# Mixer A of block 1: q and k of a head group projected together, 512 columns wide, and the latent attention's products with v one head later in the order

## The chip, the cores and the metric

One Trainium2 chip, one of its cores. The metric is the device time of one execution, in microseconds (us). The core has a matrix engine (PE, with its weight loads listed apart as PEld), a vector engine (DVE), an activation engine (ACT), a general engine (POOL) and a queue that issues transfers (SP). They run side by side and wait for each other through semaphores. Matrix products land in PSUM, which this kernel uses as eight buffers of 128x512 numbers: four named `acc`, two `mps`, two `ops`.

## The reference

Two transformer blocks in a row over 512 tokens of width 1024, in 32-bit floats. Only the first block's mixers are touched by the change:

```
proj  = rms_norm(h) @ w_in
o_a   = mixer_dilated(qkv_a) @ w_o_a       # mixer A: 3 groups of 4 heads of 64, dilations 1, 4, 16
o_b   = mixer_mla(q_c, kv_c, k_pe) @ w_o_b # mixer B, latent attention: 8 heads, full softmax
mix   = (g_a * o_a + g_b * o_b) @ w_out    # g_a, g_b: sigmoid gates from proj
h     = h + rms_norm(mix)
```

In `mixer_dilated` the q and the k of every head are turned by a rotary embedding on their first 16 of 64 numbers, each group of heads attends within a window over its own stride, and the three groups are combined by the softmax of their log-sums. In `mixer_mla` q and k have 64 plain and 32 rotary numbers a head, and each head does `softmax(q k) v` over all 512 tokens. Behind it comes an MLP (1024 to 4096 to 1024), and then the second block, with four other mixers and its own MLP.

## The kernel before

Every large product is made three times to keep its precision: each operand is split into a rounded part (hi) and the rest (lo), and `mm3` (lines 320 to 322) adds hi·hi, hi·lo and lo·hi into one PSUM buffer. Weights come from memory as units of up to 128x1024 numbers. A unit is loaded into `wraw` (3 buffers), cast by ACT into `whi` (5 buffers, line 300) and subtracted by DVE into `wlo` (5 buffers, line 301). A buffer comes free when PE has done its last product with the unit.

The change lies in `mixers1`. PE's instructions there stand in the order of the code; the other engines' instructions are placed by a scheduler when the program is built, and each engine then works in its own fixed order. The parts of `mixers1` that matter:

- `proj_v` and `proj_qk` project mixer A's v, q and k of one group. For each of the four 128-token tiles `lin_tm` makes 24 products: 8 slices of the width, 3 products each, with the tokens as the loaded operand and the weights as the streamed one, 256 columns wide. ACT copies the result out with a scale into `tm` (line 852), POOL applies the rotary embedding, and later PE transposes it, two 128x128 pieces a tile (line 860) into an `mps` buffer. After every second tile ACT and DVE copy one half each of that buffer into qT or kT (line 867).
- `ItemA` is one step of mixer A's attention: scores (lines 971 to 978), softmax, `turn` (transposes of P into `mps`, line 1014, and their copy to PT) and `out` (products with v, line 1032).
- `ItemB` is one head's 128 queries in the latent attention: `scores` (line 1092), a maximum on DVE (line 1095), an exponential on ACT (line 1099), a scale on DVE (line 1101), `turn` (four transposes, line 1106, and a copy to PT by DVE for the even head and ACT for the odd one, line 1107), and `out` (line 1122), which does both heads of a pair when the odd one comes.
- `fill` interleaves blocks of projections between these items. A block's transposes run two blocks after it (`Fill(2)`).

The loop at the end of `mixers1` steps through 16 items of A and 32 of B. At item n it issues the scores, then some blocks of fill, then the turn of an earlier item and the products with v of one earlier still. For B the turn is two items behind, and `out` three.

Of the kernel before, what the change touches and what calls it, by code (L numbers as in the profile page):

```python
# [15 lines left out]
AF = mybir.ActivationFunctionType  # L16
# [17 lines left out]
def _units():  # L34

    u = {}
    qkv = {"q": 0, "k": 768, "v": 1536}

    def rows(k0, n):
        return [128 * (k0 + i) for i in range(n)]  # L40

    for g in range(3):
        for nm in ("q", "k", "v"):
            c = list(range(qkv[nm] + 256 * g, qkv[nm] + 256 * g + 256))
            if nm == "v" and g == 0:
                c += list(range(3072, 3104))
            for h, (k0, n) in enumerate(TMK[len(c)]):
                u[f"A{nm}{g}", h] = ("w_in", rows(k0, n), c)
    for m in range(6):
        u["Bz", m] = ("w_in", rows(0, 8), list(range(2304 + 128 * m, 2432 + 128 * m)))  # L50
    heads = lambda hs, w, c0, n: [w * h + c0 + i for h in hs for i in range(n)]
    u["uqr"] = ("mla_w_uq", rows(0, 4), heads(range(8), 96, 64, 32))
    u["uv"] = ("mla_w_ukv", rows(0, 2), heads(range(8), 128, 64, 64))
    for p in range(4):
        u["uq", p] = ("mla_w_uq", rows(0, 4), heads((2 * p, 2 * p + 1), 96, 0, 64))
        u["uk", p] = ("mla_w_ukv", rows(0, 2), heads((2 * p, 2 * p + 1), 128, 0, 64))
    for m in range(16):
        u["G", m] = ("w_in", rows(0, 8), list(range(3104 + 128 * m, 3232 + 128 * m)))
    for q in range(2):
        u["oa", q] = ("w_o_a", rows(0, 2), list(range(512 * q, 512 * q + 512)))  # L60
    for q in range(4):
        u["ob", q] = ("w_o_b", rows(0, 4), list(range(256 * q, 256 * q + 256)))
    def output(nm, w, ks):

        for f in range(2):
            for i in range(0, len(ks), 2):
                u[nm, f, i // 2] = (w, [128 * k for k in ks[i:i + 2]], list(range(512 * f, 512 * f + 512)))

    def grouped(nm, w, sizes):

        for g, n in enumerate(sizes):
            k0 = sum(sizes[:g])
            if g + 1 < len(sizes):
                output((nm, g), w, range(k0, k0 + n))
            else:
                for k in range(n):
                    u[(nm, g), k] = (w, rows(k0 + k, 1), list(range(D)))

    output("out", "w_out", range(8))
    for m in range(32):  # L80
        u["ff1", m] = ("w_ff1", rows(0, 8), list(range(128 * m, 128 * m + 128)))
    grouped("ff2", "w_ff2", FF1)

    for nm, c0 in (("s5u", 0), ("hq", 256), ("hf", 512), ("fq", 1280), ("fk", 1536), ("mq", 2052), ("mk", 2308)):
        for m in range(2):
            u[nm, m] = ("w_in_2", rows(0, 8), list(range(c0 + 128 * m, c0 + 128 * m + 128)))
    for nm, c0 in (("hi", 768), ("hg", 1024), ("fv", 1792), ("mv", 2564), ("mo", 2820)):
        c = list(range(c0, c0 + 256))
        if nm == "hi":
            c += list(range(2048, 2052)) + list(range(3076, 3084))  # L90
        for h, (k0, n) in enumerate(TMK[len(c)]):
            u[nm, h] = ("w_in_2", rows(k0, n), c)
    output("out2", "w_out_2", (0, 1, 2, 3, 6, 7, 4, 5))
    for m in range(22):
        u["gate", m] = ("w_ffn_gate_2", rows(0, 8), list(range(128 * m, 128 * m + 128)))
        u["up", m] = ("w_ffn_up_2", rows(0, 8), list(range(128 * m, 128 * m + 128)))
    grouped("down", "w_ffn_down_2", FF2)
    return u
# [123 lines left out]
def program(ctx: ExitStack, tc: tile.TileContext, A, out):  # L222
# [15 lines left out]
    @contextmanager  # L238
    def phase(name, **bufs):
        with ExitStack() as st:  # L240
            CTX.bufs = bufs
            for a, n in (("cp", "c"), ("sp", "s"), ("up", "u")):
                setattr(CTX, a, st.enter_context(tc.tile_pool(name=f"{n}_{name}", bufs=1, reuse_waits="tile")))
            yield

    def u(nm="u", dt=F32, tag="u"):
        if tag in GLOBAL:
            return gpool.tile([128, 512], dt, name=nm, tag=tag, bufs=GLOBAL[tag])
        return CTX.up.tile([128, 512], dt, name=nm, tag=tag, bufs=CTX.bufs[tag])
# [4 lines left out]
    def mps():  # L254
        return psum.tile([128, 512], F32, name="mps", tag="mps", bufs=2)
# [59 lines left out]
    def wrows(nm, n, eng=DVE):  # L315
        return ktiles([wload([(nm, h)], eng=eng)[0] for h in range(len(TMK[n]))], 0, n)
# [153 lines left out]
    def lin_tm(ps, xs, pick, w, c0, n):  # L470

        K = len(xs)
        for k in range(K):
            wh, wl = w[k]
            xh, xl = pick(xs[k][0]), pick(xs[k][1])
            mm3(ps, (xh, xl), (wh[:, c0:c0 + n], wl[:, c0:c0 + n]), k == 0, k == K - 1)
# [216 lines left out]
    def tokpick(j):  # L693
        return lambda a: a[:, 128 * j:128 * j + 128]
# [95 lines left out]
    def mixers1(xs, zs, r_tm, rho, RX, rp, maskb):  # L790
# [48 lines left out]
                    gather_v(g)  # L839
                yield turn  # L840

        def proj_qk(g, nm):
            us = wrows(f"A{nm}{g}", 256)
            res = QKV[g][nm] = [u(f"{nm}T", tag="g"), u(f"{nm}T", tag="g")]
            tps = {}
            for j in range(4):
                ps = acc()
                lin_tm(ps[:, 0:256], xs, tokpick(j), us, 0, 256)
                if j % 2 == 0:
                    tt = u("tm")  # L850
                t = tt[:, 256 * (j % 2):256 * (j % 2) + 256]
                ACT.activation(t, ps[:, 0:256], AF.Copy, scale=r_tm[:, j:j + 1])
                rope(t.rearrange("p (h d) -> p h d", h=4)[:, :, 0:16], rp("ropeA", j, 32), 16, POOL)

                def turn(j=j, t=t):
                    if j % 2 == 0:
                        tps[j] = mps().rearrange("p (a x) -> p a x", a=2)
                    tpv = tps[j - j % 2]
                    for a in range(2):
                        PE.transpose(tpv[:, a, 128 * (j % 2):128 * (j % 2) + 128], t[:, 128 * a:128 * a + 128], ident)  # L860
                    if j % 2:
                        for a in range(2):
                            dst, src = res[a][:, 128 * (j - 1):128 * (j + 1)], tpv[:, a]
                            if g:
                                dst = res[a].rearrange("p (r x) -> p r x", r=4)[:, :, 32 * (j - 1):32 * (j + 1)]
                                src = src.rearrange("p (x r) -> p r x", r=4)
                            (ACT.copy if a == 0 else DVE.tensor_copy)(dst, src)
                yield turn


# [278 lines left out]

        order = [0, 8, 1, 9, 2, 10, 3, 11, 4, 12, 5, 13, 6, 14, 7, 15]  # L1150
        for g in range(3):
            fill.plan.extend([proj_v(g), proj_qk(g, "q"), proj_qk(g, "k")])
        fill.plan.extend([mixed([proj_qr(), proj_vb()], (0, 0, 1, 0, 1, 0, 1, 1)), proj_pair(0)] + [gate(m, "g") for m in order[0:2]])
        fill(14)
        rows_b()
        shared_k()
        items = [ItemA(0, j, e) for j in range(4) for e in range(2)]
        items += [ItemA(g, j, e) for g in (1, 2) for j in (0, 2) for e in range(2)]
        items += [ItemB(p, i, e) for p in range(4) for i in range(4) for e in range(2)]
        fills = [2, 1, 2, 1, 2, 1, 2, 1] + [3] * 4 + [4, 4, 3, 2]  # L1160
        fills += [0] * 32
        turned = outed = 0
        for n in range(len(items) + 4):
            if n < len(items):
                if n >= 16 and (n - 16) % 8 == 0:
                    p = (n - 16) // 8
                    if p < 3:
                        fill.plan.append(proj_pair(p + 1))
                    else:
                        fill.plan.extend(gate(m, "z") for m in order[2:14])  # L1170
                if n >= 16:
                    items[n].scores()
                elif n % 2 == 0:
                    items[n].scores(items[n + 1])
                fill(fills[n] if n < 16 else 1 if n % 8 in (1, 3) or n >= 40 and n % 2 else 0)
            if n == 24:
                combine_a()
            lag = 1 if n < 16 else 2
            while turned < len(items) and turned <= n - lag:
                items[turned].turn()  # L1180
                turned += 1
            while outed < turned and outed <= n - lag - 1:
                items[outed].out()
                outed += 1
                if outed == 16:
                    weights_a()
# [1033 lines left out]
               [lambda: po.scaled(pre.r)])  # L2220

    hd = [dram.tile([T, D], F32, name=f"hd{i}") for i in range(3)]
    with phase("m1", u=10, z=12):
        carry = mix1(hd[0])
    s5 = S5()
    with phase("f1", u=3, hid=14, s5=6):
# [21 lines left out]
```

## Time and profile before

| | |
|---|---|
| median of 3 runs | 1525.47 us (1524.91 to 1526.32) |
| the profiled execution | 1524.67 us |
| its span, first to last instruction | 1522.9 us |
| PE busy | 1478.0 us, 97% |
| DVE, ACT, POOL busy | 52%, 38%, 16% |
| granted clock, mean | 0.989 |

The profile is of one execution. A row of the timeline gives the start and the length of an instruction, or of several alike. Matrix products are pipelined, so the lengths of neighbours overlap, and what one costs is the distance from its start to the next one's start. In square brackets stands how long the engine sat idle before the row, and what ended that. In the windows, each engine's busy time has its number of instructions behind it.

### The profile page before, as it was taken

The numbers are of one execution on the slowest core, as the hardware profiler recorded it, in microseconds if no ns is written. First come the engines' busy times: TensorE is split into PE (matmuls) and PEld (weight loads), VectorE is DVE, ScalarE is ACT, GpSimd is POOL, SyncE is SP. The second block draws the span as 40 slices with busy tenths as digits, with TensorE's granted clock in tenths as the row PEclk, the third lists the DMA queues.
The fourth block names the chain that finished last, engine by engine and source line by source line (L and its number), as shares of the span: only waits on it lengthen the run. The fifth ranks groups of instructions, "written<-read, shape, count | busy, mean of one in ns | idle before, by whom it ended". The sixth has DMA issues, their size and how long they took to land.

```text
span 1522.9 us, 21857 instructions
## 1 busy us (share of the span) xinstructions
PE 1478.0 (97%) x8516; PEld 1240.6 (81%) x8520; DVE 788.6 (52%) x1569; ACT 583.7 (38%) x1099; POOL 246.2 (16%) x514
## 2 busy tenths in 40 slices
PE   8999999999999999999998999889999999999997
PEld 7999976678888888888887999667788888888885
DVE  6433367743746533434446686857656441434446
ACT  7344454533325442423225343533535323222222
POOL 0321210000201377203700052411000000000000
PEclk9999999999999999999999999979999999999999
DMA  8332121022225332322324423001124322423232
GB/s 302 132 100 75 45 64 42 33 80 97 90 91 179 119 97 70 119 85 87 110 93 141 146 88 116 32 29 42 42 90 161 124 97 59 136 83 111 83 97 84
DMA packets 54728, 147.37 MB, mean 97 GB/s; under 512 B 9824, under 2 KB 16368, under 8 KB 54624
## 3 DMA queue, kind: packets, MB, share of 16 engines
q1 hardware_dynamic: 52384, 143.38, 28.8%
q10 hardware_dynamic: 1776, 1.85, 0.4%
q8 instruction: 67, 1.10, 0.3%
q0 software_dynamic: 464, 0.74, 0.2%
q14 instruction: 37, 0.30, 0.1%
HBM read 135.12 MB, written 11.06 MB: 96 GB/s over the span
## 4 chain that ended last, share of the span: by engine, by line
PE 87%; DVE 9%; ACT 3%; issue 1%; DMA 1%; SPq 0%; DVEq 0%; ACTq 0%
PE acc L320 25%; PE acc L321 24%; PE acc L322 24%; DVE wlo L301 1%; PE acc L1092 1%; PE ops L1032 1%; PE ops L1122 1%; DVE y L625 1%; PE ops L320 1%; PE ops L322 1%; PE ops L321 1%; ACT whi L300 1%; PE acc L1977 1%; PE ops L1993 1%; PE acc L978 1%
## 5 line engine op out<-in xcount | busy, mean ns | idle before, releaser
L300 ACT CAST whi<-wraw 128x1024 fp32r<-128x1024 f32 (+4 forms) x237 | 234.5, 993 | 486.3 <-PE acc L321 226.6
L301 DVE TENSOR_TENSOR wlo<-wraw,whi 128x1024 fp32r<-128x1024 f32 (+4 forms) x237 | 282.2, 1195 | 233.7 <-ACT whi L300 224.1
L320 PE MATMUL acc<-xh,whi 128*128 128x512 f32 (+1 forms) x920 | 348.4, 380 | 7.2 <-ACT whi L300 5.3
L322 PE MATMUL acc<-xh,wlo 128*128 128x512 f32 (+1 forms) x920 | 343.5, 374 | 1.5 <-DVE wlo L301 1.5
L321 PE MATMUL acc<-xl,whi 128*128 128x512 f32 (+1 forms) x920 | 344.6, 375 | 0.3 <-DVE xl L664 0.3
L320 PEld LDWEIGHTS acc<-xh,whi 128*128 128x128 f32 x920 | 174.4, 190 | 44.1 <-ACT whi L300 7.5
L322 PEld LDWEIGHTS acc<-xh,wlo 128*128 128x128 f32 x920 | 174.2, 189 | 33.3 <-DVE wlo L301 2.1
L321 PEld LDWEIGHTS acc<-xl,whi 128*128 128x128 f32 x920 | 174.6, 190 | 31.7 <-issue 1.0
L320 PE MATMUL acc<-whi,hidh 128*128 128x512 f32 x432 | 169.0, 394 | 0.0
L321 PE MATMUL acc<-wlo,hidh 128*128 128x512 f32 x432 | 168.7, 393 | 0.0
L322 PE MATMUL acc<-whi,hidl 128*128 128x512 f32 x432 | 168.4, 392 | 0.0
L320 PE MATMUL acc<-whi,xh 128*128 128x256 f32 (+2 forms) x448 | 131.3, 293 | 0.2 <-ACT mv L1779 0.2
L321 PE MATMUL acc<-wlo,xh 128*128 128x256 f32 (+2 forms) x448 | 127.9, 285 | 0.0
L322 PE MATMUL acc<-whi,xl 128*128 128x256 f32 (+2 forms) x448 | 127.7, 285 | 0.0
L321 PEld LDWEIGHTS acc<-wlo,hidh 128*128 128x128 f32 x432 | 81.2, 188 | 18.3
L322 PEld LDWEIGHTS acc<-whi,hidl 128*128 128x128 f32 x432 | 81.2, 188 | 18.1
L320 PEld LDWEIGHTS acc<-whi,hidh 128*128 128x128 f32 x432 | 81.2, 188 | 17.9
L320 PEld LDWEIGHTS acc<-whi,xh 128*128 128x128 f32 x448 | 86.1, 192 | 2.8 <-issue 1.1
L321 PEld LDWEIGHTS acc<-wlo,xh 128*128 128x128 f32 x448 | 86.2, 192 | 0.1
L322 PEld LDWEIGHTS acc<-whi,xl 128*128 128x128 f32 x448 | 86.0, 192 | 0.0
L1252 POOL TENSOR_TENSOR relu<-relu 128x512 f32<-128x512 f32 (+1 forms) x37 | 36.9, 1005 | 230.6 <-ACT hidh L1251 226.5
L597 DVE TENSOR_TENSOR y<-acc,y 128x512 f32<-128x512 f32 x48 | 33.1, 689 | 63.1 <-PE acc L322 62.9
(535 smaller groups left out, 2151.9 us busy)
## 6 DMA issues: line engine op xcount, KB each, us to landing
wraw<-in_wp_dram SPq DMA_DIRECT2D x211, 512.0 KB, 3.5
hd<-y SPq DMA_DIRECT2D x24, 256.0 KB, 3.9
hr<-hd SPq DMA_DIRECT2D x12, 512.0 KB, 5.1
hr<-in_xt_dram SPq DMA_DIRECT2D x8, 512.0 KB, 5.5
H<-in_xT_dram SPq DMA_DIRECT2D x8, 256.0 KB, 4.6
wraw<-in_wp_dram SPq DMA_DIRECT2D x16, 128.0 KB, 3.7
gain<-in_gv_dram SPq DMA_DIRECT2D x8, 256.0 KB, 4.1
out_dram<-y SPq DMA_DIRECT2D x8, 256.0 KB, 2.1
```

The lines of the kernel that those rows point to most:

```text
L300: ACT.copy(hi[:, s], raw[:, s])
L301: eng.tensor_tensor(lo[:, s], raw[:, s], hi.bitcast(F32)[:, s], op=OP.subtract)
L320: PE.matmul(ps, lhsT=w[0], rhs=x[0], start=first, stop=False)
L321: PE.matmul(ps, lhsT=w[0], rhs=x[1], start=False, stop=False)
L322: PE.matmul(ps, lhsT=w[1], rhs=x[0], start=False, stop=last)
L597: DVE.tensor_tensor(y, ps, y, op=OP.add)
L625: DVE.scalar_tensor_tensor(y, y, self.r[:, i:i + 1], self.hs[i][:, 512 * f:512 * f + 512], op0=OP.mult, op1=OP.add)
L978: PE.matmul(Sv[:, jj, a], lhsT=QKV[g]["q"][a][rr, 128 * j:128 * j + 128], rhs=QKV[g]["k"][a][rr, k0:k0 + W], start=False, stop=(jj == step ...
L1032: PE.matmul(po[:, j % 2, h], lhsT=PTv[0:w, jj, a, b], rhs=QKV[g]["v"][v][0:w, 64 * h:64 * h + 64], start=(b == 0), stop=(b == self.nb - 1))
L1092: PE.matmul(S, lhsT=qT[2 * p + e][0:96, 128 * i:128 * i + 128], rhs=kT[2 * (p % 2) + e][0:96], start=True, stop=True)
L1122: PE.matmul(po[64 * f:64 * f + 64, 128 * i:128 * i + 128], lhsT=VB[kt][:, 64 * h:64 * h + 64], rhs=PT[:, 128 * kt:128 * kt + 128], start=F ...
L1252: POOL.tensor_tensor(a, a, a, op=OP.mult)
```

## The change

Four things change in the program, and the number of columns multiplied stays the same.

1. The weights of q and k of a group are packed side by side. Where q and k had two units each (four width slices of 256 columns), the pair now has four units (two width slices of 512 columns), with the same bytes in all.
2. `proj_qk` runs once a group. Each tile makes 24 products of 512 columns, one ACT copy of 128x512, one rotary step on eight heads, four transposes, and four copies of 128x128, ACT and DVE in turn, from one `mps` buffer.
3. The counts of `fill` follow, so that the same projections stand between the same items.
4. In the latent attention `out` comes four items behind in place of three, with one more buffer of 128x512 (`u`, 10 to 11) to hold the waiting PT, and one more step at the end of the loop.

```
         for g in range(3):
-            for nm in ("q", "k", "v"): ...
+            for h in range(4):
+                u[f"Aqk{g}", h] = ("w_in", rows(2 * h, 2), cols("q") + cols("k"))
...
-        def proj_qk(g, nm):
-            us = wrows(f"A{nm}{g}", 256)
+        def proj_qk(g):
+            us = ktiles([wload([(f"Aqk{g}", h)])[0] for h in range(4)], 0, 512)
...
             for j in range(4):
                 ps = acc()
-                lin_tm(ps[:, 0:256], xs, tokpick(j), us, 0, 256)
+                lin_tm(ps, xs, tokpick(j), us, 0, 512)
+                t = u("tm")
+                ACT.activation(t, ps, AF.Copy, scale=r_tm[:, j:j + 1])
+                rope(t.rearrange("p (h d) -> p h d", h=8)[:, :, 0:16], rp("ropeA", j, 32), 16, POOL)
...
                 def turn(j=j, t=t):
+                    tp = mps().rearrange("p (a x) -> p a x", a=4)
+                    for a in range(4):
+                        PE.transpose(tp[:, a], t[:, 128 * a:128 * a + 128], ident)
+                    for a in range(4):
+                        dst, src = res[a][:, 128 * j:128 * j + 128], tp[:, a]
...
+                        (DVE.tensor_copy if a % 2 else ACT.copy)(dst, src)
...
-            fill.plan.extend([proj_v(g), proj_qk(g, "q"), proj_qk(g, "k")])
+            fill.plan.extend([proj_v(g), proj_qk(g)])
...
-        fill(14)
+        fill(10)
...
-        fills = [2, 1, 2, 1, 2, 1, 2, 1] + [3] * 4 + [4, 4, 3, 2]
+        fills = [1] * 8 + [2] * 4 + [4, 4, 3, 2]
...
-        for n in range(len(items) + 4):
+        for n in range(len(items) + 5):
...
-            while outed < turned and outed <= n - lag - 1:
+            while outed < turned and outed <= n - lag - (1 if n < 16 else 2):
...
-    with phase("m1", u=10, z=12):
+    with phase("m1", u=11, z=12):
```

On PE, in the first q projection (tm is the copied-out block, mps the PSUM buffer of its transposes), before:

```order
L320 MATMUL acc<-whi,xh 128x256
L321 MATMUL acc<-wlo,xh 128x256
L322 MATMUL acc<-whi,xl 128x256
L860 MATMUL mps<-cstt,tm 128x128 x2
L320 MATMUL acc<-whi,xh 128x256
L321 MATMUL acc<-wlo,xh 128x256
```

and now:

```order
L322 MATMUL acc<-whi,xh 128x512
L323 MATMUL acc<-wlo,xh 128x512
L324 MATMUL acc<-whi,xl 128x512
L859 MATMUL mps<-cstt,tm 128x128 x4
L322 MATMUL acc<-whi,xh 128x512
L323 MATMUL acc<-wlo,xh 128x512
```

A block of 24 products is twice as wide, and four transposes follow it in place of two; there are half as many blocks and as many transposes in all.

On PE, in the latent attention, at two heads without a block between them (L1092 scores, L1106 transposes of P into mps, L1122 products with v; a PT is the copy of the mps that is numbered one lower), before:

```order
L1092 MATMUL acc_3133<-kT_525,qT_2831 128x512
L1106 MATMUL mps_3142<-cstt_72,P_3081 128x128 x4
L1092 MATMUL acc_3149<-kT_524,qT_2828 128x512
L1106 MATMUL mps_3158<-cstt_72,P_3112 128x128 x4
L1122 MATMUL ops_3123<-PT_3117,vb_518 64x128
L1122 MATMUL ops_3123<-PT_3143,vb_518 64x128
```

and at two heads now:

```order
L1090 MATMUL acc_2801<-kT_524,qT_2472 128x512
L1104 MATMUL mps_2810<-cstt_72,P_2764 128x128 x4
L1090 MATMUL acc_2817<-kT_525,qT_2475 128x512
L1104 MATMUL mps_2826<-cstt_72,P_2780 128x128 x4
L1120 MATMUL ops_2791<-PT_2769,vb_518 64x128
L1120 MATMUL ops_2791<-PT_2785,vb_518 64x128
```

Before, the products with v took PT_3143, whose transposes (mps_3142) stand two rows ahead of them; now they take PT_2785, whose transposes (mps_2784) stand one head further back, ahead of all these rows.

On DVE, ahead of the first scores of group 2 (mps to kT and qT are the copies of q's and k's transposes, rope and tm belong to the latent attention's q), before:

```order
L867 COPY kT<-mps 128x4x64
L688 TENSOR_TENSOR rope<-tm,ropes 128x128
L689 TENSOR_TENSOR rope<-tm,ropes 128x4x16
L690 TENSOR_TENSOR rope<-tm,ropes 128x4x16
L688 TENSOR_TENSOR rope<-tm,ropes 128x128
L689 TENSOR_TENSOR rope<-tm,ropes 128x4x16
L690 TENSOR_TENSOR rope<-tm,ropes 128x4x16
L691 TENSOR_TENSOR tm<-rope 128x128
L1017 COPY PT<-mps 128x512
L867 COPY kT<-mps 128x4x64
```

and now:

```order
L865 COPY kT<-mps 128x4x32
L690 TENSOR_TENSOR rope<-tm,ropes 128x128
L691 TENSOR_TENSOR rope<-tm,ropes 128x4x16
L692 TENSOR_TENSOR rope<-tm,ropes 128x4x16
L690 TENSOR_TENSOR rope<-tm,ropes 128x128
L691 TENSOR_TENSOR rope<-tm,ropes 128x4x16
L692 TENSOR_TENSOR rope<-tm,ropes 128x4x16
L865 COPY qT<-mps 128x4x32
L693 TENSOR_TENSOR tm<-rope 128x128 x2
L690 TENSOR_TENSOR rope<-tm,ropes 128x128
L691 TENSOR_TENSOR rope<-tm,ropes 128x4x16
L865 COPY kT<-mps 128x4x32
```

The copies are half as large and twice as many, and two of every tile's four stand on DVE between the rotary steps.

Beyond `mixers1`, PE, ACT, POOL and SP keep their order; on DVE the scheduler moved a few instructions in the second block's mixers: the first `cz` product (line 1764) after a chain of small `rsq` steps now stands ahead of most of that chain.

## Rows read from the trace of the kernel before

**Rows 1.** The page: busy time of each engine.
```profile
PE 1478.0 (97%) x8516; PEld 1240.6 (81%) x8520; DVE 788.6 (52%) x1569; ACT 583.7 (38%) x1099; POOL 246.2 (16%) x514
```

**Rows 2.** Windows (stretch; its length; busy time of each engine; clock, DMA).
```profile
55.00:216.00 161.00, 159.66 (x1256) 149.02 (x1254) 58.25 (x133) 72.08 (x201) 35.04 (x102) 1.00 0.26 81
216.00:319.00 103.00, 98.19 (x626) 68.19 (x630) 76.92 (x175) 51.53 (x104) 5.35 (x5) 1.00 0.13 45
...
253.67:267.64 13.97, 11.96 (x83) 7.28 (x83) 12.44 (x31) 8.06 (x17) 0.00 (x0) 1.00 0.11 38
276.71:290.32 13.61, 12.06 (x83) 7.28 (x83) 12.14 (x31) 8.12 (x17) 0.00 (x0) 1.00 0.11 39
```

**Rows 3.** PE's waits: for whom, us in total, times, longest.
```profile
PE ops L1122 <- ACT PT L1107: 3.0, 6, 0.8
...
PE mps L1106 <- DVE P L1101: 1.1, 3, 0.4
...
PE mps L1014 <- DVE kT L867: 0.5, 1, 0.5
```

**Rows 4.** Timeline of PE: start, length; blocks of 24 products, and transposes.
```profile
73.34 0.38 PE L860 MATMUL mps<-cstt,tm 128*128 128x128 f32 x2
73.48 0.36 PE L320 MATMUL acc<-whi,xh 128*128 128x256 f32 x1
...
76.44 0.38 PE L860 MATMUL mps<-cstt,tm 128*128 128x128 f32 x2
...
318.86 0.50 PE L320 MATMUL acc<-xh,whi 128*128 128x512 f32 x1
...
324.45 0.39 PE L320 MATMUL acc<-xh,whi 128*128 128x512 f32 x1
```

**Rows 5.** Timeline of PE in the latent attention, pairs of heads.
```profile
261.56 1.09 PE L1122 MATMUL ops<-PT,vb 128*64 128x128 f32 x14 [0.69 <-ACT PT L1107]
...
264.84 0.60 PE L1106 MATMUL mps<-cstt,P 128*128 128x128 f32 x4
...
266.62 1.09 PE L1122 MATMUL ops<-PT,vb 128*64 128x128 f32 x14 [0.82 <-ACT PT L1107]
267.64 1.12 PE L1092 MATMUL acc<-kT,qT 96*128 96x512 f32 x2
...
289.30 1.09 PE L1122 MATMUL ops<-PT,vb 128*64 128x128 f32 x14 [0.31 <-ACT PT L1107]
...
294.48 1.02 PE L1092 MATMUL acc<-kT,qT 96*128 96x512 f32 x2
295.34 0.60 PE L1106 MATMUL mps<-cstt,P 128*128 128x128 f32 x4
295.87 1.09 PE L1122 MATMUL ops<-PT,vb 128*64 128x128 f32 x16
296.89 1.12 PE L1092 MATMUL acc<-kT,qT 96*128 96x512 f32 x2
```

**Rows 6.** Timeline of ACT beside the pair at 264.84 us.
```profile
265.23 0.78 ACT L1099 ACTIVATE P<-acc,mxb,rq 128x512 f32<-128x512 f32 x1 [2.95 <-DVE mxb L1096]
...
266.00 0.57 ACT L1107 COPY PT<-mps 128x512 f32<-128x512 f32 x1
```

**Rows 7.** DVE's copies out of mps: a group, and one in the timeline.
```profile
L907 DVE COPY qr<-mps 128x128 f32<-128x128 f32 x4 | 1.1, 286 | 0.1
...
171.04 0.42 DVE L867 COPY qT<-mps 128x256 f32<-128x256 f32 x1 [5.43 <-ACT qT L867]
```

**Rows 8.** Casts and splits of weights, 55 to 216 us: busy, mean ns, idle before.
```profile
L300 ACT CAST whi<-wraw 128x1024 fp32r<-128x1024 f32 x17 | 17.8, 1049 | 6.8 <-PE acc L322 6.7
...
L301 DVE TENSOR_TENSOR wlo<-wraw,whi 128x1024 fp32r<-128x1024 f32 x18 | 22.1, 1232 | 50.9 <-ACT whi L300 50.9
```

**Rows 9.** Timeline of PE in the second block's mixers.
```profile
993.46 1.98 PE L1897 MATMUL acc<-hE 64*64 64x64 f32 x62 [3.92 <-DVE cz L1764]
```

More of the change, by code (lines that the diff above doesn't have):

```diff
@@ L42, in _units @@
     for g in range(3):
[L43 to L48, printed above, removed]
+        cols = lambda nm: list(range(qkv[nm] + 256 * g, qkv[nm] + 256 * g + 256))
+        for h in range(4):
+            u[f"Aqk{g}", h] = ("w_in", rows(2 * h, 2), cols("q") + cols("k"))
+        c = cols("v")
+        if g == 0:
+            c += list(range(3072, 3104))
+        for h, (k0, n) in enumerate(TMK[len(c)]):
+            u[f"Av{g}", h] = ("w_in", rows(k0, n), c)
     for m in range(6):
@@ L840, in proj_v @@
                 yield turn
-        def proj_qk(g, nm):
-            us = wrows(f"A{nm}{g}", 256)
-            res = QKV[g][nm] = [u(f"{nm}T", tag="g"), u(f"{nm}T", tag="g")]
-            tps = {}
+        def proj_qk(g):
+            us = ktiles([wload([(f"Aqk{g}", h)])[0] for h in range(4)], 0, 512)
+            for nm in ("q", "k"):
+                QKV[g][nm] = [u(f"{nm}T", tag="g"), u(f"{nm}T", tag="g")]
+            res = QKV[g]["q"] + QKV[g]["k"]
             for j in range(4):
                 ps = acc()
-                lin_tm(ps[:, 0:256], xs, tokpick(j), us, 0, 256)
[L849 to L853, printed above, removed]
-                def turn(j=j, t=t):
[L856 to L867, printed above, removed]
@@ new lines, in proj_qk @@
+                lin_tm(ps, xs, tokpick(j), us, 0, 512)
+                t = u("tm")
+                ACT.activation(t, ps, AF.Copy, scale=r_tm[:, j:j + 1])
+                rope(t.rearrange("p (h d) -> p h d", h=8)[:, :, 0:16], rp("ropeA", j, 32), 16, POOL)
+                def turn(j=j, t=t):
+                    tp = mps().rearrange("p (a x) -> p a x", a=4)
[3 more added lines that the diff above has]
+                        dst, src = res[a][:, 128 * j:128 * j + 128], tp[:, a]
+                        if g:
+                            dst = res[a].rearrange("p (r x) -> p r x", r=4)[:, :, 32 * j:32 * j + 32]
+                            src = src.rearrange("p (x r) -> p r x", r=4)
+                        (DVE.tensor_copy if a % 2 else ACT.copy)(dst, src)
```

## The prediction

> **What bounds the kernel now.** I read the page's busy line first: PE is busy 1478.0 us, 97% of the span; no other engine passes 52% [rows 1]. What shortens PE's own work therefore shortens the span, and what makes it wait lengthens it. Next I read the windows of the two stretches that the change touches [rows 2]. From 55 to 216 us (mixer A) PE is busy 159.66 of 161.00 us, so only 1.3 us there are visible idling. From 216 to 319 us (mostly latent attention) 4.8 of 103.00 us are. Inside that second stretch lie two shorter ones, 253.67 to 267.64 and 276.71 to 290.32 us, where no projection block stands between the heads; there DVE is busy 12.44 of 13.97 us and 12.14 of 13.61, more than PE. PE's waits name the cause: the products with v (line 1122) wait six times, 3.0 us in all, for ACT's copy of PT, and the transposes of P (line 1106) three times, 1.1 us, for DVE's P; the transposes of mixer A wait once, 0.5 us, for a kT copy [rows 3]. Last I read PE's timeline for what a block and a pair of heads cost from start to start, since lengths of neighbours overlap [rows 4, 5].
>
> Durations are of one profiled execution, 1524.67 us (span 1522.9, with 1.8 around it). The median of the runs is 1525.47, so 0.8 us are added at the end.
>
> **Wider blocks of q and k.** What goes: 24 blocks (3 groups, q and k, 4 tiles) of 24 products of 256 columns. One takes from 73.48 to 76.44 us, 2.96 us [rows 4], 0.123 a product. What comes: 12 blocks of 24 products of 512 columns. The stretch before has 512-column blocks elsewhere: from 318.86 to 324.45, 24 products, 5.59 us, 0.233 each [rows 4]. Twice 2.96 less 5.59 is 0.33; over 12 blocks that is 4.0. I take -3.7, because some of the narrow blocks' first products already lie beside transposes. The bounds are -4.0 and, were the 512-column form to cost just twice a narrow block, 0.
>
> So a fixed 13 ns or so of each product goes with 288 products fewer (2 x 0.123 - 0.233). The Trainium skill, on the page "TensorE: Matmul & The Clock Gate", section "Wait — 56ns, not 53.3ns?", gives a fixed cost of about 2.5 ns a product beyond its columns; by it this term would be an estimated 288 x 2.5 ns = 0.7 us. The blocks of [rows 4] have a larger one, and the measurement decides.
>
> **Transposes.** Two stand ahead of a narrow block and cost it 0.14 us (73.34 to 73.48 [rows 4]); 24 such pairs are 3.4. Now four stand behind each of 12 wide blocks. Four in a row ahead of products with v cost 0.53 (295.34 to 295.87 [rows 5]), so the 12 lie between 12 x 0.28 = 3.4 and 12 x 0.53 = 6.4: 0 to +3.0. What follows them here is a block, as in the cheap row, so I take 0.35 each, 4.2, or +0.8.
>
> **Copies of the transposes.** Before, a buffer was emptied by two halves, one on ACT and one on DVE; now by four copies of 128x128, ACT and DVE in turn. DVE's copy at 171.04 us had waited, idle, for ACT's copy out of the same buffer to end [rows 7]: they go one after the other. A 128x128 copy takes 0.286 [rows 7], so the chain of four takes 4 x 0.286 plus some hops of 0.04 (an estimate), 1.25 us, against 2 x 0.42 = 0.84 before. Mid-group a block of 5.6 us on PE covers it. It shows where a group's first scores follow the last turn, at groups 1 and 2, where two of each tile's copies also queue on DVE between rotary steps of the latent attention's q. Bounds: 0 (covered) and 2 x 1.25 = +2.5 (all exposed); I take the excess at both joints, 2 x 0.41 = +0.8.
>
> The rule that speaks against this edit is in the Trainium skill, "PSUM — Partial Sum Buffer", section "PSUM bank collisions raise a hardware error": two engines must not touch the same quadrant of a bank at once, readers included, so the accesses are kept apart by dependencies. The trace agrees by the row at 171.04. With the copies side by side the chain would be 0.6 and this term below 0.
>
> The one wait of mixer A's transposes for DVE's kT copy was behind two-tile batches; with smaller copies and half the blocks it should go, -0.5 [rows 3]; it may stay (0).
>
> **The products with v, one head later.** A pair of heads that meets no wait takes, from the second head's transposes through the products with v to the next scores, 295.34 to 296.89, 1.55 us; the pair at 264.84 takes until 267.64, 2.80 [rows 5]. So 1.25 are lost, of which 0.82 are marked as a wait. What holds it is ACT: its exponential started only at 265.23, having stood 2.95 us for DVE's maximum, and the PT copy came behind it, 266.00 to 266.57 [rows 6]. With the products one head later, this copy has one head more to land; its cost on this path is gone.
>
> How much comes back? In the stretch 253.67 to 267.64 PE does six transposes, five scores, three sets of products with v. At 0.53, 0.86 (294.48 to 295.34) and 1.02 (295.87 to 296.89) [rows 5] that is 10.5 us and 13.97 were taken: 3.4 lost. The other stretch holds the same instructions (83) and 13.61: 3.1 lost. But what is late next is DVE, which has 12.44 and 12.14 us of work there, so unless it falls behind without harm, PE can't get below these: the gain is 1.53 and 1.47, or -3.0 together. The transposes of an item two heads back wait for its P from DVE, and as `mps` has two buffers also for the PT copy two back. The four marked waits of the two stretches (0.69 at 261.56, 0.82 at 266.62, 0.31 at 289.30 [rows 5], and one more like the first) are 2.5 of the 3.0 us; the other two, of 0.5 together, lie after the last scores. For those and the first round, where DVE's P was waited for as well, I take -1.0. Sum -4.0. Bounds: -1.5 (half of the marked waits, the rest turning up before the transposes) and -7.5 (all 6.5 and the 1.0).
>
> What one head more costs: the last PT needs one more step at the end, with no block to cover it, priced within the -1.0.
>
> **Elsewhere.** On DVE the first `cz` product moves ahead of most small `rsq` steps in block 2. PE stood 3.92 us for `cz` at 993.46 [rows 9]. How long those steps take isn't in my rows; a few tenths each at most, so I take -0.7, between +0.3 (later for some other reason) and -1.5.
>
> **Weights.** A group's q and k use four units of 128x1024 together, where before q's two were freed while k's were in use. There are five `whi` buffers, so the next group's casts start later. ACT's casts already stood 6.8 us for PE's last use [rows 8], and still PE lost only 1.3 us in the whole stretch [rows 2]: blocks of v and queued scores covered it. In the new order a unit's last use comes at a quarter, a half, three quarters and the end of the group's last block, 1.4 us apart, while a cast takes 1.05; I cost it at nothing, and the third rival is what it costs without the cover.
>
> **Sum.** -3.7 + 0.8 + 0.8 - 0.5 - 4.0 - 0.7 = -7.3: 1517.4 for the profiled execution, 1518.2 for the median. Its own range is 1515 to 1521.
>
> **Rivals.**
> First: DVE takes over as the bound and the wait moves from the products with v to the transposes (or to the scores, for a free buffer). For it: DVE is busy 89% of both short stretches [rows 2], and PE waits for its P three times already [rows 3]. Against it: a wait for P only shows after DVE has used its slack, and the blocks between give it some. Then this part gives 1.5 in place of 4.0: 1520.7.
>
> Second: the copies at the joints, with their turn-taking, and the dearer transposes use up what the wide blocks save; mixer A's terms sum to 0 in place of -2.6. For it: the turn-taking in [rows 7]; against it, 5.6 us of cover mid-group. 1520.8.
>
> Third, slower: the weight buffers. ACT stands in a cast for a unit that PE still uses; behind it in its queue stand the evacuations of `acc`, exponentials and PT copies, and PE's block then waits for its own units. Per group boundary, two casts and a split come after the release and before the block: 2 x 1.05 + 1.23 = 3.3 us [rows 8]; four boundaries (into and out of groups 1 and 2) are 13.3. It decides from the point where a unit comes free later than one block before PE needs the next. For it: the 6.8 us of waiting casts; against it: PE's 1.3 us of idling [rows 2]. -7.3 + 13.3 = +6.0: 1531.5.
>
> That the change doesn't do what it says is excluded for PE's order, which shows both; that both of the first two rivals come together leaves -2.2, 1523.3.
>
> **How the numbers follow.** Forecast 0.60, first rival 0.17, second 0.13, third 0.06, the first two together 0.04. No change means within 0.2%, 3.05 us, about what a measurement of this kernel tells: 1522.4 to 1528.5. The forecast and the first two rivals lie below it; taking a fifth of each rival and a few of the forecast as falling short, faster is 0.81, no change 0.12, slower 0.07. The range goes from 1513 (mixer B's lower bound with the rest as taken would give 1514.7, wide blocks at their best a little less) to 1523.5, which takes in the first two rivals; the third lies outside.
>
> **What would show it.** In the profile after: 12 blocks of 24 products of 512 columns at about 5.6 us; mixer A's stretch some 2.6 us shorter, and where it isn't, PE waits at the first scores of groups 1 and 2 for copies into kT or qT. No waits of the products with v for ACT's PT; the two short stretches at about 12.4 and 12.1 us, with larger waits of the transposes for P if the first rival holds. The wait for `cz` at about 3.2. Casts that wait for PE followed by PE waiting for `whi` or `wlo` would show the third rival. The prediction is wrong if mixer A's stretch grows, or the latent attention's stays at its 103 us.

## The result, and the profile after

The changed kernel takes 1516.94 us (median of 5 runs, 1514.97 to 1521.59), the kernel before 1525.15 in the same comparison (5 runs, 1524.91 to 1526.32): a ratio of 0.9937, 95% interval 0.9915 to 0.9958. The forecast was 1518.2, between 1513.0 and 1523.5. In a later comparison it was 1514.94 against 1526.18, 0.9922 (0.9910 to 0.9934). The profiled execution took 1515.25, with a span of 1513.5.

The page of the kernel after has this line of busy time, to be read against [rows 1]:

```profile
PE 1469.6 (97%) x8228; PEld 1222.3 (81%) x8232; DVE 788.9 (52%) x1581; ACT 582.7 (38%) x1099; POOL 233.2 (15%) x466
```

PE has 288 instructions fewer and 8.4 us less work; its share of the span is the same. To see where the time went I cut each trace at three points of PE that every kernel here has: the first product of the first v block (288 columns), the first scores of the latent attention, and the first product behind the last products with v. Part A lies between the first two, part B between the second and the third, and the rest reaches to the end of the span. The windows of the three parts, first of the kernel before, then after (columns as in [rows 2]):

```profile
39.62:216.53 176.91, 175.57 (x1379) 164.89 (x1378) 68.00 (x186) 79.39 (x216) 38.18 (x114) 1.00 0.26 82
216.53:318.86 102.33, 97.52 (x620) 67.52 (x624) 76.42 (x174) 51.19 (x104) 4.82 (x5) 1.00 0.13 44
318.86:1522.90 1204.04, 1170.61 (x6377) 979.99 (x6376) 619.77 (x1158) 425.39 (x724) 201.98 (x389) 0.99 0.30 97
```

```profile
40.71:215.21 174.50, 172.38 (x1092) 149.48 (x1090) 69.50 (x198) 78.30 (x216) 24.93 (x66) 1.00 0.27 83
215.21:311.49 96.28, 92.61 (x621) 65.40 (x624) 75.53 (x174) 51.35 (x104) 5.41 (x5) 1.00 0.15 48
311.49:1513.50 1202.01, 1169.57 (x6378) 978.89 (x6376) 619.85 (x1158) 425.30 (x724) 201.62 (x389) 0.99 0.30 97
```

Part A is 2.4 us shorter, B 6.05, the rest 2.0. Against that stands a start that came 1.1 us later (39.62 and 40.71), before the first instruction that was changed; in the experiments, two with the old q and k blocks among them, it lies between 40.4 and 42.3, so the profile of before had an early one. The sum is -9.4, the difference of the spans.

In part B only 1.1 of the 6.05 us come off PE's idle time (102.33 - 97.52 = 4.81 before, 96.28 - 92.61 = 3.67 after). The other 4.9 come off its busy time, though the products are the same: part of what the waits cost stands as busy in these windows.

The waits of PE in the kernel after, those that answer to [rows 3] and [rows 9]:

```profile
PE mps L1104 <- DVE mxb L1094: 2.7, 3, 1.1
PE acc L1895 <- DVE cz L1762: 2.2, 1, 2.2
...
PE mps L1012 <- DVE rope L692: 1.4, 1, 1.4
...
PE mps L1104 <- DVE P L1099: 0.4, 1, 0.4
```

No product with v waits for ACT's PT any more. The transposes of the latent attention wait for DVE instead, 3.1 us where it was 1.1, and the transposes of mixer A have a new wait of 1.4.

The names in these rows need care. Transposes read P, which DVE scales, and nothing of mxb. Timelines of DVE and PE after:

```profile
254.71 0.48 DVE L1099 TENSOR_SCALAR P<-P,rl 128x512 f32<-128x512 f32 x1
255.10 0.21 DVE L1094 TENSOR_SCALAR mxb<-mxb,rq 128x1 f32<-128x1 f32 x1
```

```profile
255.33 0.63 PE L1104 MATMUL mps<-cstt,P 128*128 128x128 f32 x4 [0.81 <-DVE mxb L1094]
```

The scale of P ends at 255.19 and PE goes on 0.14 us later, the distance that it also has where the row names P (scale to 259.74, transposes at 259.88 in the kernel before). The mxb that is named only happens to end in between. So all 3.1 us are waits for P, and the wait that names `rope` is one for the kT copy ahead of it, as shown below.

### The profile page after: what moved, and what is told of

Same layout as the page of the kernel before. It is cut to its first block, busy times and chain, and to the rows that moved or that the text cites. A ratio compares the mean times of both kernels' runs of the same rounds, so it can differ in the third digit from the quotient of the medians.

```text
span 1513.5 us, 21231 instructions
## 1 busy us (share of the span) xinstructions
PE 1469.6 (97%) x8228; PEld 1222.3 (81%) x8232; DVE 788.9 (52%) x1581; ACT 582.7 (38%) x1099; POOL 233.2 (15%) x466
## 5 line engine op out<-in xcount | busy, mean ns | idle before, releaser
L322 PE MATMUL acc<-whi,xh 128*128 128x256 f32 (+3 forms) x352 | 113.8, 323 | 0.2 <-ACT mv L1777 0.2
L323 PE MATMUL acc<-wlo,xh 128*128 128x256 f32 (+3 forms) x352 | 111.1, 316 | 0.0
L324 PE MATMUL acc<-whi,xl 128*128 128x256 f32 (+3 forms) x352 | 111.0, 315 | 0.0
L322 PEld LDWEIGHTS acc<-whi,xh 128*128 128x128 f32 x352 | 67.5, 192 | 6.3 <-issue 1.1
L324 PEld LDWEIGHTS acc<-whi,xl 128*128 128x128 f32 x352 | 67.5, 192 | 3.9
L323 PEld LDWEIGHTS acc<-wlo,xh 128*128 128x128 f32 x352 | 67.5, 192 | 3.5
```

The source lines that it names most:

```text
L322: PE.matmul(ps, lhsT=w[0], rhs=x[0], start=first, stop=False)
L323: PE.matmul(ps, lhsT=w[0], rhs=x[1], start=False, stop=False)
L324: PE.matmul(ps, lhsT=w[1], rhs=x[0], start=False, stop=last)
```

## The experiments

All lengths of parts below are from windows cut as above; before has A 176.91, B 102.33, rest 1204.04, and after 174.50, 96.28, 1202.01. PE's mean granted clock over the span stands beside a rest where it matters.

**The wide blocks alone.** The changed kernel, with the products with v back at three items behind (the last step of the loop and the extra buffer of `u` go back with them):

```
-            while outed < turned and outed <= n - lag - (1 if n < 16 else 2):
+            while outed < turned and outed <= n - lag - 1:
```

> The wide q and k blocks alone; the products with v stay where they were before. Theory (the two edits act apart): mixer A's stretch is 2.4 us shorter, as in the changed kernel, the latent attention as long as before with its four long waits for ACT's PT copy, and the earlier cz product (this build has it) gives some 2 us more: about 1520.8 us. Rival (the wide blocks also set the latent attention going, so that part of its gain is theirs): 1517 to 1519, and the waits for PT are fewer than six.

Measured: 1523.72 us (1521.42 to 1528.80), ratio 0.9988 (0.9975 to 1.0001). Part A 174.52, B 102.39, rest 1202.16 at a clock of 0.990. That is 2.9 above the expected 1520.8: the runs went from 1521.42 at a clock of 0.990, the profiled one, to 1528.80 at 0.984. The parts decide: A is all of the changed kernel's gain there, B has none of it. PE's waits in part B are those of before:

```profile
PE ops L1120 <- ACT PT L1105: 3.0, 6, 0.8
PE mps L1104 <- DVE P L1099: 1.1, 3, 0.4
```

**The later products alone.** The kernel before, with only the order changed (and with it the extra buffer of `u` and the last step; what the buffer does by itself isn't told apart):

```
-            while outed < turned and outed <= n - lag - 1:
+            while outed < turned and outed <= n - lag - (1 if n < 16 else 2):
```

> The later products with v alone; q and k in narrow blocks as before. Theory (the edits act apart): mixer A's stretch as before, the latent attention 5.9 us shorter with no wait for PT, and the earlier cz product (this build has it too) some 2 us: about 1517.3 us. Rival (the latent attention gains only together with the wide blocks): 1520 or more. If both kernels with one part each hold the cz gain, their two gains add up to more than the whole change gives.

Measured: 1518.77 us (1518.02 to 1519.86), ratio 0.9946 (0.9930 to 0.9961). A 176.94, B 96.43, rest 1202.93 at 0.989. The time is 1.5 above the expected 1517.3; the rest gave 1.1 of the 2 us that were put on it. So the two edits act apart: -2.4 in A by one, -5.9 in B by the other, and their sum is what the change gives there. The waits in part B:

```profile
PE mps L1106 <- DVE mxb L1096: 2.8, 3, 1.2
PE mps L1106 <- DVE P L1101: 0.3, 1, 0.3
```

**Is it DVE that was late?** Both kernels with the row maximum of the latent attention left out, and with it two of DVE's instructions a head (a reduction of 0.69 us and a small product of 0.21):

```
-                mx = small(1, "mxb", 6)
-                DVE.tensor_reduce(mx, S, axis=AX.X, op=OP.max)
-                DVE.tensor_scalar(mx, mx, rq[:, i:i + 1], -1.0, op0=OP.mult, op1=OP.mult)
...
-                ACT.activation(self.P, S, AF.Exp, scale=rq[:, i:i + 1], bias=mx, accum_out=l)
+                ACT.activation(self.P, S, AF.Exp, scale=rq[:, i:i + 1], accum_out=l)
```

> The kernel before with the row maximum of the latent attention left out (the exponential gets no bias): two DVE instructions a head less. Theory (the products with v waited because DVE's maximum came late and held up ACT's exponential, and with it the PT copy behind it): most of the 3.0 us of waits for PT go and the latent attention gets 4 to 6 us shorter by this alone, 1517 to 1520 us with the cz gain. Rival (ACT's own order and work hold the copy up): the waits for PT stay at 2 us or more and the time stays above 1522.

> The changed kernel with the same maximum left out. Theory: with DVE relieved the products with v have nothing left to gain from coming later, so this differs from the kernel before without the maximum by mixer A's 2.4 us and at most 1.5 more: 2.4 to 3.9 us lower. Rival (ACT's order is the limit, and only the later products lift it): the difference stays at 6 us or more.

Measured: 1517.18 us for before without the maximum (ratio to before 0.9938, 0.9922 to 0.9954), 1514.39 for after without it (0.9920, 0.9903 to 0.9938). Part B is 94.60 and 92.53, with PE, DVE and ACT busy as here, first before, then after:

```profile
218.11:312.71 94.60, 93.55 (x620) 66.53 (x623) 52.88 (x110) 49.19 (x104) 4.96 (x5) 1.00 0.14 48
```

```profile
215.06:307.59 92.53, 91.94 (x620) 65.77 (x623) 52.88 (x110) 49.16 (x104) 5.52 (x5) 1.00 0.14 50
```

Of the waits for ACT's PT 0.5 us was left in the one, at the last two sets of products, and none in the other. So part of what stood at ACT was made by DVE's maximum: 2.5 of the 3.0 us at most, 1.3 if ACT's order, below, is taken off. Part B got 7.7 us shorter by this alone, more than the 4 to 6 expected. With the maximum the later products are worth 6.05 us in part B, without it 2.07, a little over the 1.5 that I allowed.

ACT's order was not held fixed, though. In the kernel before, a copy for qT stands between an exponential and the PT copy that PE waits 0.69 us for, twice (the products at 261.56 and at 284.75). Timeline of ACT at the second:

```profile
283.52 0.58 ACT L926 COPY qT<-acc 64x512 f32<-64x512 f32 x1
284.11 0.59 ACT L1107 COPY PT<-mps 128x512 f32<-128x512 f32 x1
```

In the changed kernel, in the later products alone and without the maximum the scheduler puts that PT copy first; in the wide blocks alone the order is that of before. So up to 2 x 0.58 = 1.2 us (an estimate from this row) of what part B gained can be ACT's new order, which no run tells apart from the distance.

**The new wait in mixer A.** In the kernel after PE waits at 179.90 us. Timeline of PE there (products left out):

```profile
176.03 0.60 PE L859 MATMUL mps<-cstt,tm 128*128 128x128 f32 x4
...
177.90 0.60 PE L859 MATMUL mps<-cstt,tm 128*128 128x128 f32 x4
...
179.90 0.63 PE L1012 MATMUL mps<-cstt,P 128*128 128x128 f32 x4 [1.40 <-DVE rope L692]
```

Timeline of DVE beside it, from the wlo split that waited for its cast:

```profile
176.24 1.22 DVE L303 TENSOR_TENSOR wlo<-wraw,whi 128x1024 fp32r<-128x1024 f32 x1 [2.06 <-ACT whi L302]
177.38 0.28 DVE L865 COPY kT<-mps 128x128 f32<-128x128 f32 x1
177.58 0.28 DVE L690 TENSOR_TENSOR rope<-tm,ropes 128x128 f32<-128x128 f32 x1
...
178.53 0.28 DVE L865 COPY qT<-mps 128x128 f32<-128x128 f32 x1
...
179.46 0.29 DVE L865 COPY kT<-mps 128x128 f32<-128x128 f32 x1
```

The copies of 0.28 us are short; what takes the time is that rotary steps of the latent attention's q stand between them in DVE's queue, six before the qT copy alone. ACT's copies of the same buffers wait for DVE's in turn. The last kT copy ends at 179.75, and PE goes on 0.15 us later; the `rope` that its row names ends in between. To tell the queue from the copies' own chain, all four went to ACT:

```
-                        (DVE.tensor_copy if a % 2 else ACT.copy)(dst, src)
+                        ACT.copy(dst, src)
```

> The changed kernel with all four copies of each q and k tile's transposes on ACT. Theory (the 1.4 us that the transposes of P wait at 179 us come from DVE's queue: the copies there stand behind rotary steps of the latent attention's q): that wait goes, and mixer A's stretch is 3.9 us shorter than before in place of 2.4. Rival (the copies' own chain is the price: four in a row from one buffer): four on one engine still take some 1.2 us, and a wait of 1 us or more stays there. In this build the cz product stands late, as in the kernel before: what lies behind the first block's mixers should come back to before's length (theory: the 2 us there are due to cz and the clock), so the time would be some 1517.

Measured: 1516.69 us (1515.42 to 1520.81), ratio 0.9942 (0.9926 to 0.9958). The wait is gone and A is 173.14, 3.8 us shorter than before. The four copies of that tile take 0.77 us on ACT (176.47 to 177.24), so four in a row aren't the price: DVE's queue between them was the cause. Whether the handing to and fro between the engines adds something without rotary steps wasn't run. The rest, with the cz product late as in before (PE waits 3.9 us for it), is 1204.02 at before's clock of 0.989, before's 1204.04. So the 2 us of the rest hang on cz and the clock.

A build in which only the last tile's copies moved to ACT kept cz early:

```
-                        (DVE.tensor_copy if a % 2 else ACT.copy)(dst, src)
+                        (DVE.tensor_copy if a % 2 and not (g == 2 and j > 2) else ACT.copy)(dst, src)
```

> The changed kernel with the four copies of the last q and k tile of group 2 on ACT, all others as they were. Theory (only that tile's copies stand behind DVE's rotary steps where PE needs the buffer): mixer A's stretch 3.8 us shorter than before as with all copies on ACT, and as the cz product stands early in this build, the part behind the mixers 1 to 2 us shorter than before too: 1.4 us below the changed kernel. Rival (the copies on ACT are needed on every tile): the 1.4 us wait stays, no gain over the changed kernel.

Measured: 1516.26 us (1514.81 to 1523.94), 0.9937 (0.9917 to 0.9957). A miss: A 174.60, and the wait stayed, 1.5 us. There are two buffers, so the transposes at 179.90 want the one that was filled at 176.03, by the tile before the last. Its copies went to ACT in the next run (`j == 2` in place of `j > 2`), which also had all PT copies on ACT, since that build again had cz early:

> The changed kernel with the copies of tile 2 of group 2's q and k on ACT (one tile earlier than the copies moved in the run of the last tile), and the PT copies of the latent attention on ACT. In this build the cz product stands early, as in the changed kernel. Theory (the transposes of P at 179 us need the buffer that the last but one tile's transposes filled, and DVE's copies of that tile stand behind rotary steps): the wait of 1.4 us goes and mixer A's stretch is 3.8 us shorter than before; with the latent attention as in the changed kernel, 1.3 us below it. Rival (it needs all copies on ACT): the wait stays.

Measured: 1515.60 us (1514.45 to 1518.98), 0.9923 (0.9906 to 0.9939). The wait at the transposes is gone, but 1.3 us came back one step later, at the first scores, which now wait for the last tile's copies:

```profile
PE acc L976 <- DVE kT L865: 1.0, 1, 1.0
...
PE acc L976 <- ACT kT L865: 0.3, 1, 0.3
```

A is 175.18, not the 3.8 us less than before that were expected, and B 96.28. Behind these waits the granted clock fell to 0.51 (183 to 185 us) and 0.64 (185 to 187), which cost an estimated 2 x 0.49 + 2 x 0.36 = 1.7 us of A. One tile alone isn't enough, the last or the one before it; both off DVE were only run with all copies on ACT.

**Is there more to gain by going later still?** One head more needs a buffer that only fits with two raw weight buffers in place of three, so there is a control with that alone.

```
-    WB = (3, 5)
+    WB = (2, 5)
...
-            while outed < turned and outed <= n - lag - (1 if n < 16 else 2):
+            while outed < turned and outed <= n - lag - (1 if n < 16 else 3):
```

> The changed kernel with two buffers for raw weights in place of three: the control for the next one, which needs the room. Some us slower than the changed kernel if a load then comes late anywhere; the mixers of block 1 within 0.5 us of it.

> The control with the products with v one more head later, five items behind (one buffer of 128x512 more). Theory (DVE now limits the latent attention, the transposes wait for it): no more to gain, its stretch within 0.7 us of the control's, and the waits for DVE's mxb and P stay at some 3 us. Rival (the PT copies still come late and hold PE back through the products): 2 us or more shorter. The cz product stands late here and early in the control, which is worth 1 to 2 us against this one behind the first block's mixers.

Measured: 1533.54 us for the control (1528.36 to 1538.71), 1536.58 one head later (1535.02 to 1540.73). The control's part A was 180.40, not within 0.5 of 174.50: two more waits of some 1.1 us for kT copies, and a clock of 0.98; its profile is of its slowest run. Its B is 96.60, as it should be. One head later B is 103.66: neither unchanged nor shorter, but 7.1 longer. The waits there are 6.6 us where mxb is named and 0.5 for P (the control: 2.8 and 0.3), 4.0 more. Two of them are of 2.7 us, and behind each the granted clock was at its lower level (0.50 from 265 to 267 us and from 289 to 291); the part's mean clock of 0.97 makes an estimated 3 us of its 103.66, which is the remainder. One of the two, on PE and then on DVE:

```profile
263.79 0.63 PE L1104 MATMUL mps<-cstt,P 128*128 128x128 f32 x4 [2.68 <-DVE mxb L1094]
```

```profile
258.65 1.22 DVE L303 TENSOR_TENSOR wlo<-wraw,whi 128x1024 fp32r<-128x1024 f32 x1
259.78 0.21 DVE L1094 TENSOR_SCALAR mxb<-mxb,rq 128x1 f32<-128x1 f32 x1
...
262.32 0.69 DVE L1093 TENSOR_REDUCE mxb<-acc 128x1 f32<-128x512 f32 x1
...
263.17 0.48 DVE L1099 TENSOR_SCALAR P<-P,rl 128x512 f32<-128x512 f32 x1
```

The small product for the maximum stands behind a weight split of 1.22 us. The exponential follows it at 260.03, but the scale of its P comes only at 263.17, behind a later head's maximum and other copies; it ends 0.14 us before PE goes on. Each build has its own order on DVE, and this one puts more ahead of the maximum and the scale. Both the theory and the rival missed. More distance for the products doesn't pay for a worse order on DVE. How much of the 4.0 is the order and how much the distance isn't told apart.

**Relieving DVE.** The scale of P on POOL:

```
-                DVE.tensor_scalar(self.P, self.P, l, None, op0=OP.mult)
+                POOL.tensor_scalar(self.P, self.P, l, None, op0=OP.mult)
```

> The changed kernel with the scale of P by 1/l on POOL, idle in the latent attention, in place of DVE. Theory (DVE's work is what limits): the waits for mxb, 2.7 us, go, the stretch behind the combine is 1 to 3 us shorter, 1514 to 1516 us. Rival (P then arrives later by a slower POOL): the transposes wait for P from POOL instead, and the stretch is longer by 2 us or more.

Measured: 1521.15 us (1519.14 to 1521.91), 0.9965 (0.9952 to 0.9977), B 99.86. The rival held: POOL takes 1591 ns for what DVE does in 483, and the transposes wait for it:

```profile
PE mps L1104 <- POOL P L1099: 4.9, 6, 1.2
```

And every PT copy on ACT, in the kernel with the last tile's copies on ACT:

```
-                (ACT.copy if self.e else DVE.tensor_copy)(self.PT, tp)
+                ACT.copy(self.PT, tp)
```

> The kernel of the run above with every PT copy of the latent attention on ACT, where the even heads' were on DVE: three copies of 0.68 us less on DVE and three of 0.57 more on ACT in each stretch without blocks. Theory (DVE's work limits there): the transposes' waits for DVE shrink from 3 us to 1 or less and the latent attention is 1 to 2.5 us shorter. Rival (with all copies behind its exponentials ACT is late with the buffers): the transposes or products wait for ACT's PT instead, and nothing is gained or up to 3 us lost.

Measured: 1517.80 us (1514.58 to 1519.74), 0.9936 (0.9923 to 0.9950). DVE is busy 67.65 us in part B in place of 75.38, ACT 58.03 in place of 51.38, and B is 96.65 against 96.12: nothing gained, nothing lost. PE waits for DVE as long as ever, 3.2 us (2.9 without the move):

```profile
PE mps L1104 <- DVE P L1099: 2.0, 4, 0.6
PE mps L1104 <- DVE mxb L1094: 1.2, 1, 1.2
```

DVE now stands idle for ACT's P, and ACT has the copies ahead of its exponentials. Timelines of DVE and ACT:

```profile
281.27 0.16 DVE L1098 RECIPROCAL rl<-rl 128x1 f32<-128x1 f32 x1 [0.87 <-ACT P L1097]
```

```profile
281.14 0.57 ACT L1105 COPY PT<-mps 128x512 f32<-128x512 f32 x1
281.61 0.79 ACT L1097 ACTIVATE P<-acc,mxb,rq 128x512 f32<-128x512 f32 x1
```

The exponential at 281.61 had its maximum by 280.40. So DVE's sum of work alone doesn't bind there. What fits the rows is the chain through one head, maximum on DVE, exponential on ACT, scale on DVE, and whatever stands ahead of each link in its queue. The maximum left out is the only edit here that shortened part B further, and it took both a link and 23 us of work off DVE; these two aren't told apart.

**The changed kernel on that chip.** Run beside the last tile's copies and the PT copies, for comparison.

> The changed kernel itself, on the chip of the two runs above, so that they are compared on one chip: 1516 to 1518 us.

Measured: 1514.94 us (1514.38 to 1515.81), 1.1 below the expected range; A 174.46, B 96.43. Of the versions on that chip none is faster than it.

## Why the prediction came out

The time (1516.94 for 1518.2) and the sign were right, and each edit acted where it was said to. Between the two profiled executions -7.3 was forecast and -9.4 measured: part A came out as forecast, B gained 2.0 more and the rest 1.3 more. The late start took 1.1 of that back, and no edit explains it, so that part of the agreement is luck. Step by step:

- **Wide blocks**, -3.7 forecast. A block now, timeline of PE, first and next after its transposes:

```profile
67.43 0.48 PE L322 MATMUL acc<-whi,xh 128*128 128x512 f32 x1
...
72.99 0.60 PE L859 MATMUL mps<-cstt,tm 128*128 128x128 f32 x4
73.35 0.48 PE L322 MATMUL acc<-whi,xh 128*128 128x512 f32 x1
```

 That is 5.56 us a block, and all twelve take 66.7, against 24 x 2.945 = 70.7 (their mean over the trace of before): -4.0, the end of the range that I had shaved by 0.3 for no reason that the trace bore out.
- **Transposes**, +0.8: four cost 0.36 here, and 4.84 over the twelve (without waits) against 4.10 over the 24 pairs: +0.7.
- **Copies**, +0.8, and the wait that was to go, -0.5. The old wait went (-0.6). The new one costs 1.56 (177.90 to 179.90, less the 0.44 of four transposes). I had the turn-taking right and took the chain of four copies, 1.25 us, as the price; it was the rotary steps between them that made it, which I had named as a queue but not counted. I charged both joints 0.41; the trace shows 1.56 at one of them. Part A in sum: -4.0 + 0.7 - 0.6 + 1.6 = -2.3; forecast -2.6, measured -2.4. That an error of 0.7 in the copies and one of 0.3 in the blocks went opposite ways is luck.
- **Later products**, -4.0: the mechanism was right, the size too small. Measured -6.05 in part B. The waits for PT went, perhaps with some help from ACT's new order (at most 1.2, above), which the prediction leaves out, and in both short stretches DVE was what came late next. But I had called DVE's busy time there, 12.44 and 12.14 us [rows 2], a floor. The two stretches with the same instructions on PE now:

```profile
250.54:262.89 12.35, 11.04 (x84) 6.84 (x84) 11.66 (x27) 7.58 (x16) 0.00 (x0) 1.00 0.15 45
271.70:283.50 11.80, 10.85 (x83) 6.91 (x83) 10.82 (x26) 7.72 (x16) 0.00 (x0) 1.00 0.16 47
```

 They gained 1.62 and 1.81, for the 1.53 and 1.47 of the floor, and DVE has 27 and 26 instructions in them where it had 31: the others, of 174 in part B before and after, moved beside the blocks around them. More of the miss is in the end: I gave it and the first round 1.0 together. The last heads' transposes and products, timeline of PE after:

```profile
307.01 0.60 PE L1104 MATMUL mps<-cstt,P 128*128 128x128 f32 x4
307.54 1.09 PE L1120 MATMUL ops<-PT,vb 128*64 128x128 f32 x16
308.57 1.09 PE L1104 MATMUL mps<-cstt,P 128*128 128x128 f32 x8
309.59 1.97 PE L1120 MATMUL ops<-PT,vb 128*64 128x128 f32 x32
311.49 0.50 PE L322 MATMUL acc<-xh,whi 128*128 128x512 f32 x1
```

 and before (left out: the first two products of each set):

```profile
313.94 1.04 PE L1106 MATMUL mps<-cstt,P 128*128 128x128 f32 x8
...
315.49 1.09 PE L1122 MATMUL ops<-PT,vb 128*64 128x128 f32 x14 [0.16 <-ACT PT L1107]
316.51 0.66 PE L1106 MATMUL mps<-cstt,P 128*128 128x128 f32 x4
...
317.84 1.09 PE L1122 MATMUL ops<-PT,vb 128*64 128x128 f32 x14 [0.31 <-ACT PT L1107]
```

 After, three transposes (of four pieces each) and three sets of products take 4.48 us without a wait. Before, three and two took from 313.94 to 318.86 [rows 4], 4.92. With 1.02 for a set that is 1.46 gained at the end, where only 0.47 had been marked as waiting. The remaining 1.2 lie in the first round and in pairs between the stretches.
- **The cz product**, -0.7: PE's wait for it fell from 3.92 [rows 9] to 2.24 us, and part of that came back in the waits behind it, 3.8 for 3.2 us on `ssd`. At before's clock the rest was shorter by 0.4 (last tile's copies on ACT: 1203.63, with a wait of 0.6 elsewhere that before doesn't have) to 1.1 (later products alone). The 2.0 of the profiled execution hold about 1 more, which I put down to a clock of 0.990 in place of 0.989 (an estimate: 0.001 of 1202 us is 1.2).
- **The first rival** (DVE becomes the bound) was half right: the wait moved to DVE, 2.0 us more than before, and still the gain was more than forecast. **The second** (the joints eat the gain of A) had its place right and its price too high. **The third**, weights, never showed: PE's waits from 56 to 214 us name no weights.

## What to carry to other kernels

Price a wait from start to start against a pair without one; the marked idle time was 4.1 us here and 3.1 are still marked after, yet 6.05 came back. Where a wait names an instruction that the waiter doesn't read, look for the one just ahead of it. A busy engine in a window gives a floor only if its work can't slide out of the window, and moving work off it can gain nothing when the engine that takes the work is a link of the same chain. Where a copy frees a buffer, count what stands ahead of it in its engine's queue, not only its own time.

## What the runs showed of the hardware

A product of 512 columns costs less than two of 256: 0.232 us against 2 x 0.123, some 14 ns for each product fewer. The same tensor-scalar of 128x512 numbers took 1591 ns on POOL and 483 on DVE. With the products one head later still, two waits of PE of 2.7 us were each followed by a stretch at a granted clock of 0.50, the lower of its two levels, and 4.0 us of added waits came with 7.1 us of added length. And the runs of one program lay up to 7 us apart, the longer ones at the lower granted clock (1521.4 at 0.990 to 1528.8 at 0.984), more than most of the terms above, so parts of a trace, and not medians alone, told these edits apart.
